# Splitting paired weight blocks as three tiles of 1024 columns and one of 512

## The chip, the cores and the metric

The kernel runs on one core of a Trainium2 chip. The time is the device time of one execution in microseconds (us), and what is compared is the median over several executions. A core has five engines, each with an instruction queue of its own that it works through in order: TensorE for matmuls (PE, and PEld for the weight loads that run beside them), VectorE (DVE), ScalarE (ACT), GpSimd (POOL) and SyncE (SP), which here issues transfers. The engines are held in step by semaphores. Which instruction stands where in a queue is settled when the program is built: a scheduler orders each engine's instructions from the order of the code and the buffers that are free, so a change of tile sizes can also move instructions that the change does not name.

## The reference, cut

One encoder layer on x of shape (1, 512, 1024) in float32: two gated branches (retention and a spatial gating unit) and a convolutional gated MLP.

```python
x1 = x  + rmsnorm_post_mix(sig(a_ret) * (Retention(h) @ w_ret_o) + sig(a_sgu) * (SGU(h) @ w_sgu_o))
y  = x1 + rmsnorm_post_ffn(ConvGatedMLP(rmsnorm_pre_ffn(x1)))      # h = rmsnorm_pre_mix(x)

def _sgu_branch(u, sv, ...):                 # u, sv, a_ret, a_sgu: columns of h @ w_in
    u = gelu(u); sv = layernorm(gelu(sv), ...)
    y = u * (einsum('gpq,bnqgc->bnpgc', w_spatial, chunks(sv)) + b_spatial.T)
    return y @ w_sgu_o
def _conv_gated_mlp(h, w_up, conv_w, conv_b, w_down):   # w_up: 1024 -> 2 x 2816
    hid = depthwise_conv(h @ w_up, conv_w) + conv_b
    ...                                                  # gate, then @ w_down: 2816 -> 1024
```

## The kernel before

All matrices are float32. A matmul runs on values split in a high and a low part: the high part is the value rounded to the TensorE's float32 format (made by a copy on ACT, L100), the low part what is left of it (a subtraction on VectorE, L119). Three matmuls per product add high × high, high × low and low × high. `split(hi, lo, src)` issues the copy and the subtraction.

**Weights.** They come as 146 blocks of 128 × 1024 (`wall`) by transfers into raw tiles (`raw_tile`, four buffers), and are split into tiles of a pool of nine buffers, `slot`, each 128 × 1088. A list `units` says in which order the pieces are needed; `w_get` hands out the next and prepares pieces ahead, as many as fit by `w_size` (in slots) into nine.

**Pairs.** For 20 pairs of weight blocks the product of two 512-deep, 2-block matrices is formed in Strassen's way, with 7 products in place of 8. Four pairs make the SGU's u (called U pairs), eight the two gates a_ret and a_sgu (gate pairs, `GATE0` to `GATE1`), eight belong to the up projection (`COUPLES`). Seven weight forms of 128 × 512 are needed per pair, out of the four quarters: B11, B21, T1, T2, T3, T4 and B22, each used by one product of 12 matmuls of 128 × 256 columns (L926). The T forms are sums of quarters made in `w_form`: T1 (L205) and T3 (L206) on VectorE, T2 (L208) and T4 (L211) on VectorE for U and up pairs and on GpSimd for gate pairs. T2 and T4 share half a raw tile. Each form is one split, and one slot holds its high and its low part.

**The pair's products.** Class `Pair` makes them in three parts: part 1 the products with B11, B21, T1 and T2; part 2 that with T3; part 3 those with T4 and B22. The result of the first product is copied out of PSUM on ACT at once, since the fourth product of the pair adds to the same PSUM bank. Between the parts other work is put by a table, `MIDDLE`, written out by hand: a row such as `U10 W2 U20 G10 U30 G20 U11` is part 1 of U pair 0, a weight block of an output projection (W, by `f_block`, L300 to L302), part 2 of U pair 0, part 1 of gate pair 0, and so on. Part 3 is followed by the activation (gelu, sigmoid; L1052, L1061), which loads a table on ACT when the function changes.

**After the pairs** come the conv, the down projection (L1372; its weights are split in `w_down` to dh and dl), and the last norm.

Of the kernel before, what the change touches and what calls it, by code (L numbers as in the profile page):

```python
# [13 lines left out]
ALU = mybir.AluOpType  # L14

P = 128
D = 1024
S = 512
# [9 lines left out]
SV0, U0, GATE0, GATE1 = 24, 32, 40, 72  # L28
# [8 lines left out]
UP0 = DOWN0 - 2 * NF  # L37
# [15 lines left out]
def tile_block(ctx: ExitStack, tc, xT, x, wall, par, cs, wsp, bsp, gpost, gffn, out):  # L53
    nc = tc.nc
# [6 lines left out]
    def nm(s):  # L61
        uid[0] += 1
        return f"{s}_{uid[0]}"
# [35 lines left out]
    def copy(o, i):  # L99
        return nc.scalar.activation(out=o, in_=i, func=AF.Copy)  # L100

    def two(t):
        return t.rearrange("p (n c) -> p n c", n=2)
# [8 lines left out]
    def as32(t):  # L112
        return t.bitcast(F32)
# [3 lines left out]
    def split(hi, lo, src):  # L117
        copy(hi, src)
        low[0] = nc.vector.tensor_sub(lo, src, as32(hi)).ins  # L119
# [2 lines left out]

    RES1 = NW - 22 - 44
    RES0 = RES1 - RES_OUT
    FORMS = ("B11", "B21", "T1", "T2", "T3", "T4", "B22")
    units = []
    i = 0
    while i < NW:
        pair = [(f, i) for f in FORMS]
        if i == SV0:  # L130
            units += [(f, k) for f in ("s11", "sT1", "sT2") for k in range(2)]
            units += [(f, k) for k in range(2) for f in ("s22", "sT3")]
            units += [(f, k) for f in ("s21", "sT4") for k in range(2)]
            i = U0
        elif i == U0:
            us, gs = ([[(f, k + n * m) for f in FORMS] for n in range(KD // 2)] for k, m in ((U0, 2), (GATE0, 4)))
            ws = [("blk", GATE0 + 4 * (n // 2) + 2 + n % 2) for n in range(KD)]
            for what, n in MIDDLE:
                units += {"W": lambda: ws[n : n + 1], "U1": lambda: us[n][:4], "U2": lambda: us[n][4:],
                          "G1": lambda: gs[n][:4], "G2": lambda: gs[n][4:]}.get(what, list)()  # L140
            i = GATE0 + 2 * KD
        elif GATE0 <= i < GATE1:
            units += pair[:4] + [("blk", i + 2)] + pair[4:] + [("blk", i + 3)]
            i += 4
        elif i == UP0 + 2 * COUPLES[0][0]:
            for a, b in COUPLES:
                pair = [(f, UP0 + 2 * a) for f in FORMS]
                units += pair[:4] + [("blk", UP0 + 2 * b)] + pair[4:] + [("blk", UP0 + 2 * b + 1)]
# [44 lines left out]

    def w_form(form, i):

        if form == "B11":
            a, b = raw_tile(), raw_tile()
            nc.sync.dma_start(a, wall[i])
            nc.sync.dma_start(b, wall[i + 1])
            w_raw["B11"], w_raw["B12"] = a[:, :S], a[:, S:]  # L200
            w_raw["B22"], w_raw["B21"] = b[:, :S], b[:, S:]
        elif form == "T1":
            t = raw_tile()
            w_raw["T1"], w_raw["T2"], w_raw["T3"], w_raw["T4"] = t[:, :S], t[:, S:], w_raw["B12"], t[:, S:]
            nc.vector.tensor_add(w_raw["T1"], w_raw["B11"], w_raw["B12"])  # L205
            nc.vector.tensor_add(w_raw["T3"], w_raw["B12"], w_raw["B22"])  # L206
            eng = nc.vector if i < GATE0 or i >= UP0 else nc.gpsimd
            eng.tensor_tensor(out=w_raw["T2"], in0=w_raw["T1"], in1=w_raw["B22"], op=ALU.add)  # L208
        elif form == "T4":
            eng = nc.vector if i < GATE0 or i >= UP0 else nc.gpsimd  # L210
            eng.tensor_tensor(out=w_raw["T4"], in0=w_raw["T2"], in1=w_raw["B21"], op=ALU.add)  # L211
        w = slot("wf", 0, 1088)
        lo, hi = w[:, AT_64 : AT_64 + S], w[:, S + AT_192 : 2 * S + AT_192]
        split(hi, lo, w_raw[form])
        return hi, lo

    def w_down(form, i):
# [60 lines left out]
    def w_unit(u):  # L278
        return w_block(u[1]) if u[0] == "blk" else (w_down if u[0] in "qt" else w_sv if u[0][0] == "s" else w_form)(*u)

    def w_size(u):
        return 2 if u[0] in ("blk", "q", "t") or u[0][0] == "s" else 1

    def w_get(look=LOOK):

        i = w_pos[0]
        w_pos[0] += 1
        room = 2 * look + (2 if w_size(units[i]) == 2 else 0)
        n = sum(w_size(u) for u in units[i : w_pos[1]])
# [18 lines left out]
    T0, T1 = slice(0, 256), slice(256, 512)  # L308
# [95 lines left out]
    for k in range(KD):  # L404
# [9 lines left out]
        wh, wl = w_get(1 if k < 4 else LOOK if k < KD - 1 else 2)  # L414
# [12 lines left out]
        for m in QK if k == KD - 1 else range(8):  # L427
            c = slice(m * P, (m + 1) * P)
# [36 lines left out]
    for t in range(NT):  # L465
        for n in range(2):
# [3 lines left out]
                out=xt, in_=xt, func=AF.Square, accum_out=ss[:, 4 * n + t : 4 * n + t + 1]  # L470
# [54 lines left out]
    raw, swapped = {}, {}  # L525
# [383 lines left out]
    class Pair:  # L909
# [6 lines left out]
            self.b = [ps() for _ in range(3)]  # L916
            self.two = in_turn if a is None else two

        def product(self, b, act, first, w=None):
            wh, wl = w or w_get()  # L920
            o = self.b[b][:, T0]
            for k in range(4):
                c = slice(k * P, (k + 1) * P)
                h_, l_ = act(k)
                for n, (w_, a_) in enumerate(((wh, h_), (wh, l_), (wl, h_))):
                    self.last = nc.tensor.matmul(  # L926
                        o, w_[:, c], a_, start=first and k == n == 0, stop=k == 3 and n == 2,
                        skip_group_check=True,
                    )
            pe_last[0] = self.last.ins  # L930
            return self.two(o)
# [10 lines left out]
        def part1(self):  # L942

            c0, c1 = self.t

            def second():
                o = self.product(1, self.x(4, T0), True)
                self.sum = v.tensor_add(two(c0[:, T0]), o, two(c0[:, T0])).ins

            o = self.product(0, self.x(0, T0), True)  # L950
            copy(two(c0[:, T0]), o)
            second()
            self.product(2, self.s("S1"), True)
            o = self.product(0, self.s("S2"), False)
            self.copied = copy(two(c1[:, T0]), o).ins
            if self.scale is not None:
                v.tensor_mul(c0[:, T0], c0[:, T0], self.scale[:, T0])

        def part2(self):
            c0, c1 = self.t  # L960
            o = self.product(0, self.s("S3"), False)
            copy(two(c1[:, T1]), o)
            v.tensor_sub(two(c1[:, T1]), self.two(self.b[2][:, T0]), two(c1[:, T1]))
            self.w = w_get(), w_get()

        def part3(self):
            c0, c1 = self.t
# [63 lines left out]
    r, us, gs = [], {}, {}  # L1031
# [299 lines left out]
    i = 0  # L1331
    while i < NF:
        if i in couples:
            p = Pair(None, lambda: tmp("c"), (h2h, h2l, h2forms))
            p.part1()
            o = [f_block(h2h, h2l, KD)]
# [5 lines left out]
        else:  # L1342
            o = []
# [75 lines left out]
    for j in range(DP):  # L1419
# [5 lines left out]
        if j in (3, 5):  # L1425
            w = w_get()
# [152 lines left out]
def _two(a):  # L1579

    b = _parts(a, 8, P).reshape(4, 2, P, 2, S)
    return np.stack([
        np.concatenate([b[:, 0, :, 0], b[:, 1, :, 0]], -1), np.concatenate([b[:, 1, :, 1], b[:, 0, :, 1]], -1),
    ], 1)


def _up(a):

    for i, _ in COUPLES:
        b, c = a[2 * i].reshape(P, 2, S), a[2 * i + 1].reshape(P, 2, S)  # L1590
        a[2 * i : 2 * i + 2] = np.stack([
            np.concatenate([b[:, 0], c[:, 0]], -1), np.concatenate([c[:, 1], b[:, 1]], -1),
        ])
    return a


# [82 lines left out]
```

## Time and profile before

| what | us |
| --- | --- |
| median of 3 runs (lowest, highest) | 783.61 (783.21, 783.69) |
| profiled execution, span | 782.6 |
| median less the span | 1.01 |
| ACT busy | 485.2 |
| POOL busy | 103.5 |

The runs list no separate time for the profiled execution; its span, from the first to the last recorded instruction, stands for it, and the median of the runs is 1.01 us longer. In the rows of the profile, "out<-in" names tiles as the program does, without their numbers; "x140" is a count, the number after the bar is the busy time in us, then the mean of one instruction in ns, then the idle time of the engine just before, with what ended it. L100 is line 100 of the kernel before.

### The profile page before, as it was taken

Reading aid. Unit: us, or ns where it says so; the run is one execution under the profiler, and the core shown is the slowest. Engines: PE = TensorE matmul, PEld = TensorE weight load, DVE = VectorE, ACT = ScalarE, POOL = GpSimd, SP = SyncE. Lnnn points to the kernel's source line nnn. Section 1 sums busy time; section 2 is a strip of 40 time slices with the busy share of each in tenths; the row PEclk is TensorE's granted clock in tenths of the full one; section 3 lists DMA queues with packets and bytes.
Section 4 is the critical chain, followed back from the end, with each engine's and each line's share of the span. In section 5 each row is a group of like instructions: output and inputs, shape, how many; then the busy total and the mean of one; then the engine's idle time right before and its main releaser. Section 6 shows DMA issues by size and latency. Waiting matters only on the chain.

```text
span 782.6 us, 13472 instructions
## 1 busy us (share of the span) xinstructions
PE 774.5 (99%) x5139; PEld 720.7 (92%) x5139; DVE 639.5 (82%) x1093; ACT 485.2 (62%) x878; POOL 103.5 (13%) x132
## 2 busy tenths in 40 slices
PE   9999999999999999999999999999999999999996
PEld 8888998998999999999998998999999998999996
DVE  6567987789789988877765679989999889886987
ACT  7555568688466766644454686657777568644542
POOL 0040001130021102033211200001111012200001
PEclk9999999999999999999999999999999999999998
DMA  8783224453223233233459120435555375733344
GB/s 288 271 246 102 81 82 162 108 122 108 81 91 126 82 122 121 83 110 106 138 171 337 54 81 28 124 107 141 142 148 149 108 199 111 171 114 107 109 162 162
DMA packets 35889, 104.80 MB, mean 134 GB/s; under 512 B 4400, under 2 KB 6320, under 8 KB 35824
## 3 DMA queue, kind: packets, MB, share of 16 engines
q1 hardware_dynamic: 27936, 87.81, 34.0%
q0 software_dynamic: 7024, 14.95, 9.0%
q10 hardware_dynamic: 864, 1.18, 0.4%
q8 instruction: 40, 0.66, 0.4%
q14 instruction: 25, 0.20, 0.1%
HBM read 91.34 MB, written 4.19 MB: 122 GB/s over the span
## 4 chain that ended last, share of the span: by engine, by line
PE 92%; DVE 3%; DMA 3%; issue 1%; ACT 0%; POOLq 0%; DVEq 0%; POOL 0%; ACTq 0%
PE ps L926 24%; PE ps L300 12%; PE ps L302 12%; PE ps L301 12%; PE ps L1372 7%; PE ps L755 5%; PE ps L634 4%; PE ps L636 4%; PE ps L635 4%; DMA raw<-wall 3%; PE ps L1109 2%; PE ps L1108 2%; PE ps L1107 2%; DVE dl L119 1%; PE ps L997 1%
## 5 line engine op out<-in xcount | busy, mean ns | idle before, releaser
L119 DVE TENSOR_TENSOR wl<-raw,wh 128x1024 fp32r<-128x1024 f32 (+1 forms) x84 | 96.0, 1152 | 54.3 <-issue 19.1
L100 ACT ACTIVATE wf<-raw 128x512 fp32r<-128x512 f32 x140 | 85.6, 625 | 67.3 <-PE ps L301 19.4
L926 PE MATMUL ps<-sh,wf 128*128 128x256 f32 x640 | 117.4, 276 | 0.1
L119 DVE TENSOR_TENSOR wf<-raw,wf 128x512 fp32r<-128x512 f32 x140 | 107.0, 774 | 9.2 <-ACT wf L100 8.6
L926 PEld LDWEIGHTS ps<-sh,wf 128*128 128x128 f32 x640 | 101.9, 192 | 1.1 <-ACT sig L100 0.5
L100 ACT ACTIVATE wh<-raw 128x1024 fp32r<-128x1024 f32 (+2 forms) x88 | 84.8, 977 | 28.5 <-DMA raw<-wall 14.0
L300 PE MATMUL ps<-h2h,wh 128*128 128x512 f32 (+1 forms) x256 | 90.6, 354 | 0.0
L301 PE MATMUL ps<-h2l,wh 128*128 128x512 f32 (+1 forms) x256 | 90.4, 353 | 0.0
L302 PE MATMUL ps<-h2h,wl 128*128 128x512 f32 (+1 forms) x256 | 90.4, 353 | 0.0
L926 PE MATMUL ps<-sl,wf 128*128 128x256 f32 x320 | 88.0, 275 | 0.0
L926 PEld LDWEIGHTS ps<-sl,wf 128*128 128x128 f32 x320 | 61.4, 192 | 0.4
L1372 PE MATMUL ps<-dh,fh 128*128 128x256 f32 x216 | 59.6, 276 | 0.3 <-DVE yy L1409 0.3
L1372 PE MATMUL ps<-dl,fh 128*128 128x256 f32 x216 | 59.5, 275 | 0.0
L1372 PE MATMUL ps<-dh,fl 128*128 128x256 f32 x216 | 59.4, 275 | 0.0
L100 ACT ACTIVATE dh<-raw 128x768 fp32r<-128x768 f32 (+1 forms) x36 | 33.6, 950 | 33.8 <-DVE raw L231 15.2
L302 PEld LDWEIGHTS ps<-h2h,wl 128*128 128x128 f32 x256 | 48.6, 190 | 5.1
L301 PEld LDWEIGHTS ps<-h2l,wh 128*128 128x128 f32 x256 | 48.6, 190 | 4.5
L300 PEld LDWEIGHTS ps<-h2h,wh 128*128 128x128 f32 x256 | 48.6, 190 | 4.5
L926 PE MATMUL ps<-xh,wf 128*128 128x256 f32 x288 | 52.2, 275 | 0.0
L636 PE MATMUL ps<-wh,xl 128*128 128x512 f32 x128 | 48.5, 379 | 0.0
L635 PE MATMUL ps<-wl,xh 128*128 128x512 f32 x128 | 48.5, 379 | 0.0
L634 PE MATMUL ps<-wh,xh 128*128 128x512 f32 x128 | 48.5, 380 | 0.0
(343 smaller groups left out, 2171.6 us busy)
## 6 DMA issues: line engine op xcount, KB each, us to landing
raw<-wall SPq DMA_DIRECT2D x144, 512.0 KB, 3.7
x<-x SPq DMA_DIRECT2D x24, 256.0 KB, 6.0
fl<-gp POOLq DMA_DIRECT2D x12, 256.0 KB, 3.8
swap<-qkraw POOLq DMA_DIRECT2D x16, 128.0 KB, 4.8
x<-x POOLq DMA_DIRECT2D x8, 256.0 KB, 2.3
fl<-fs POOLq DMA_DIRECT2D x8, 256.0 KB, 4.3
xT<-xT SPq DMA_DIRECT2D x7, 256.0 KB, 5.0
xT<-xT POOLq DMA_DIRECT2D x4, 256.0 KB, 4.1
```

Source lines behind the costliest of these rows:

```text
L100: return nc.scalar.activation(out=o, in_=i, func=AF.Copy)
L119: low[0] = nc.vector.tensor_sub(lo, src, as32(hi)).ins
L300: nc.tensor.matmul(o, ah, bh, start=start, stop=False, skip_group_check=skip)
L301: nc.tensor.matmul(o, ah, bl, start=False, stop=False, skip_group_check=skip)
L302: pe_last[0] = nc.tensor.matmul(o, al, bh, start=False, stop=stop, skip_group_check=skip).ins
L634: nc.tensor.matmul(acc[t], xh[k][:, c], turns(wh[:, f]), start=k == 0, stop=False)
L635: nc.tensor.matmul(acc[t], xh[k][:, c], turns(wl[:, f]), start=False, stop=False)
L636: part_end[0] = nc.tensor.matmul(acc[t], xl[k][:, c], turns(wh[:, f]), start=False, stop=k == KD - 1)
L755: nc.tensor.matmul(bank[t], a_[:, c], turns(w_[:, f]), start=first and k == i == 0, stop=last and k == 3 and i == 2, skip_group_check=True,)
L926: self.last = nc.tensor.matmul(o, w_[:, c], a_, start=first and k == n == 0, stop=k == 3 and n == 2, skip_group_check=True,)
L1107: nc.tensor.matmul(o, ah, turns(bh), start=k == 0, stop=False)
L1372: nc.tensor.matmul(o, a_[:, c], turns(w_[:, f]), start=j == t == i == 0, stop=j == DP - 1 and i == 2 and n not in (M2, M3, M4), skip_group ...
```

## The change

The seven forms become four pieces: `B1` (B11 and B21 side by side), `T12`, `T34` and `B22`. The first three are raw tiles of 128 × 1024 that are split whole, with a slot for the high and one for the low part; B22 stays as it was. A pair still takes seven slots. The host lays out the blocks so that B11 and the quarter of the second product stand side by side. T2 is summed on VectorE in all pairs (L206 after the change), T3 and T4 go into the first raw tile once B1 is split (L209, L210 after). T4 stays on GpSimd for gate pairs. A product no longer fetches its weights: `halves` fetches a tile for two products, and in part 2 the second half of T34 is kept for part 3.

```diff
-    FORMS = ("B11", "B21", "T1", "T2", "T3", "T4", "B22")
+    FORMS = ("B1", "T12", "T34", "B22")
...
-                units += {"W": lambda: ws[n : n + 1], "U1": lambda: us[n][:4], "U2": lambda: us[n][4:],
-                          "G1": lambda: gs[n][:4], "G2": lambda: gs[n][4:]}.get(what, list)()
+                units += {"W": lambda: ws[n : n + 1], "U1": lambda: us[n][:2], "U2": lambda: us[n][2:],
+                          "G1": lambda: gs[n][:2], "G2": lambda: gs[n][2:]}.get(what, list)()
...
-            units += pair[:4] + [("blk", i + 2)] + pair[4:] + [("blk", i + 3)]
+            units += pair[:2] + [("blk", i + 2)] + pair[2:] + [("blk", i + 3)]
...
     def w_form(form, i):
 
-        if form == "B11":
-            a, b = raw_tile(), raw_tile()
+        eng = nc.vector if i < GATE0 or i >= UP0 else nc.gpsimd
+        if form == "B1":
+            a, b = w_raw["a"], w_raw["b"] = raw_tile(), raw_tile()
             nc.sync.dma_start(a, wall[i])
             nc.sync.dma_start(b, wall[i + 1])
-            w_raw["B11"], w_raw["B12"] = a[:, :S], a[:, S:]
-            w_raw["B22"], w_raw["B21"] = b[:, :S], b[:, S:]
-        elif form == "T1":
-            t = raw_tile()
-            w_raw["T1"], w_raw["T2"], w_raw["T3"], w_raw["T4"] = t[:, :S], t[:, S:], w_raw["B12"], t[:, S:]
-            nc.vector.tensor_add(w_raw["T1"], w_raw["B11"], w_raw["B12"])
-            nc.vector.tensor_add(w_raw["T3"], w_raw["B12"], w_raw["B22"])
-            eng = nc.vector if i < GATE0 or i >= UP0 else nc.gpsimd
-            eng.tensor_tensor(out=w_raw["T2"], in0=w_raw["T1"], in1=w_raw["B22"], op=ALU.add)
-        elif form == "T4":
-            eng = nc.vector if i < GATE0 or i >= UP0 else nc.gpsimd
-            eng.tensor_tensor(out=w_raw["T4"], in0=w_raw["T2"], in1=w_raw["B21"], op=ALU.add)
-        w = slot("wf", 0, 1088)
-        lo, hi = w[:, AT_64 : AT_64 + S], w[:, S + AT_192 : 2 * S + AT_192]
-        split(hi, lo, w_raw[form])
+            w_raw["B22"], w_raw["B12"] = b[:, :S], b[:, S:]
+            raw = a
+        elif form == "T12":
+            raw = w_raw["t"] = raw_tile()
+            nc.vector.tensor_add(raw[:, :S], w_raw["a"][:, :S], w_raw["B12"])
+            nc.vector.tensor_add(raw[:, S:], raw[:, :S], w_raw["B22"])
+        elif form == "T34":
+            raw = w_raw["a"]
+            nc.vector.tensor_add(raw[:, :S], w_raw["B12"], w_raw["B22"])
+            eng.tensor_tensor(out=raw[:, S:], in0=w_raw["t"][:, S:], in1=raw[:, S:], op=ALU.add)
+        if form == "B22":
+            w = slot("wf", 0, 1088)
+            lo, hi = w[:, AT_64 : AT_64 + S], w[:, S + AT_192 : 2 * S + AT_192]
+            raw = w_raw["B22"]
+        else:
+            hi, lo = slot("wf", AT_192), slot("wf", AT_64)
+        split(hi, lo, raw)
         return hi, lo
...
     def w_size(u):
-        return 2 if u[0] in ("blk", "q", "t") or u[0][0] == "s" else 1
+        return 1 if u[0] == "B22" else 2
...
+        def halves(self):
+            hi, lo = w_get()
+            return [(hi[:, f], lo[:, f]) for f in (slice(0, S), slice(S, 2 * S))]
...
-            o = self.product(0, self.x(0, T0), True)
+            w = self.halves()
+            o = self.product(0, self.x(0, T0), True, w[0])
             copy(two(c0[:, T0]), o)
-            second()
-            self.product(2, self.s("S1"), True)
-            o = self.product(0, self.s("S2"), False)
+            second(w[1])
+            w = self.halves()
+            self.product(2, self.s("S1"), True, w[0])
+            o = self.product(0, self.s("S2"), False, w[1])
...
         def part2(self):
             c0, c1 = self.t
-            o = self.product(0, self.s("S3"), False)
+            w = self.halves()
+            o = self.product(0, self.s("S3"), False, w[0])
             copy(two(c1[:, T1]), o)
             v.tensor_sub(two(c1[:, T1]), self.two(self.b[2][:, T0]), two(c1[:, T1]))
-            self.w = w_get(), w_get()
+            self.w = w[1], w_get()
```

TensorE runs the same matmuls in the same order but for one place: three matmuls of an output projection (yh with wh and wl, L300 to L302 before), which stood ahead of the fourth product of the gate pair whose results are sig_645 and sig_646, stand behind it. On the other engines the order moves in many places; three are shown. Names with numbers are tiles; the second number is a running count and differs between the two programs.

The first place is ScalarE in the middle of that gate pair. The copy sig_645<-ps_647 brings the pair's first result out of PSUM; L1061 before and L1071 after is the sigmoid of an earlier pair. Before:

```order
L100 ACTIVATE wf_633_3599<-raw_617_3456 128x512
L100 ACTIVATE wf_634_3603<-raw_621_3491 128x512
L100 ACTIVATE yh_641_3657<-u_585_3248 128x512
L100 ACTIVATE wf_650_3670<-raw_618_3457 128x512
L1061 ACT_TABLE_LOAD
L1061 ACTIVATE sig_611_3435<-sig_611_3435 128x512
L100 ACTIVATE yh_643_3661<-u_586_3249 128x512
L1061 ACTIVATE sig_612_3436<-sig_612_3436 128x512
L100 ACTIVATE sig_645_3665<-ps_647_3667 128x256
```

After the change, the same stretch of ScalarE:

```order
L100 ACTIVATE wf_633_3548<-raw_617_3421 128x1024
L100 ACTIVATE yh_641_3603<-u_585_3206 128x512
L100 ACTIVATE wf_650_3616<-raw_618_3422 128x512
L100 ACTIVATE sig_645_3611<-ps_647_3613 128x256
L1071 ACT_TABLE_LOAD
L1071 ACTIVATE sig_611_3387<-sig_611_3387 128x512
L1071 ACTIVATE sig_612_3388<-sig_612_3388 128x512
```

The copy now stands ahead of the table load and the sigmoids, and the copies of two weight forms are one.

The second place is ScalarE in part 1 of the third U pair (results u_535 and u_536); L1052 before and L1062 after is the gelu of the second U pair. Before:

```order
L1052 ACT_TABLE_LOAD
L1052 ACTIVATE u_490_2565<-u_490_2565 128x512
L100 ACTIVATE sig_518_2759<-ps_519_2760 128x256
L100 ACTIVATE wf_533_2883<-raw_514_2751 128x512
L1052 ACTIVATE u_491_2566<-u_491_2566 128x512
L100 ACTIVATE wf_534_2887<-raw_523_2779 128x512
L100 ACTIVATE u_535_2890<-ps_537_2892 128x256
```

After, on ScalarE at the same place:

```order
L1062 ACT_TABLE_LOAD
L1062 ACTIVATE u_490_2547<-u_490_2547 128x512
L100 ACTIVATE sig_515_2728<-ps_516_2729 128x256
L1062 ACTIVATE u_491_2548<-u_491_2548 128x512
L100 ACTIVATE u_535_2860<-ps_537_2862 128x256
L100 ACTIVATE wf_533_2856<-raw_519_2732 128x1024
```

The copies of two forms, which stood ahead of the copy u_535<-ps_537, became one that stands behind it.

The third place is VectorE around the first weight tile of the second U pair. wf_475 and wf_481 are that pair's forms B11 and B21 before; wf_481 alone is the low part of its B1 after. raw_482 is where its T1 and T2 are summed, and wf_467, wf_468, wf_471 and wf_472 belong to the gate pair ahead of it. Before:

```order
L119 TENSOR_TENSOR wf_467_2378<-raw_465_2357,wf_467_2378 128x512
L119 TENSOR_TENSOR wf_468_2381<-raw_461_2322,wf_468_2381 128x512
L119 TENSOR_TENSOR wf_471_2414<-raw_465_2357,wf_471_2414 128x512
L963 TENSOR_TENSOR u_456_2302<-ps_459_2305,u_456_2302 128x256
L119 TENSOR_TENSOR wf_472_2431<-raw_462_2323,wf_472_2431 128x512
L119 TENSOR_TENSOR wf_475_2438<-raw_473_2434,wf_475_2438 128x512
L205 TENSOR_TENSOR raw_482_2462<-raw_473_2434 128x512
L119 TENSOR_TENSOR wf_481_2446<-raw_474_2435,wf_481_2446 128x512
L206 TENSOR_TENSOR raw_473_2434<-raw_473_2434,raw_474_2435 128x512
```

After, on VectorE from the gate pair's T3 sum (L209) to the low part of B1:

```order
L209 TENSOR_TENSOR raw_461_2329<-raw_462_2330 128x512
L119 TENSOR_TENSOR wf_467_2367<-raw_465_2363,wf_466_2366 128x1024
L119 TENSOR_TENSOR wf_471_2402<-raw_461_2329,wf_470_2401 128x1024
L205 TENSOR_TENSOR raw_482_2461<-raw_478_2427,raw_479_2428 128x512
L206 TENSOR_TENSOR raw_482_2461<-raw_482_2461,raw_479_2428 128x512
L973 TENSOR_TENSOR u_456_2296<-ps_459_2299,u_456_2296 128x256
L955 TENSOR_TENSOR sig_473_2422<-ps_476_2425,sig_473_2422 128x256
L966 TENSOR_TENSOR sig_473_2422<-sig_473_2422,rbc_103_567 128x256
L119 TENSOR_TENSOR wf_472_2405<-raw_462_2330,wf_472_2405 128x512
L119 TENSOR_TENSOR wf_481_2432<-raw_478_2427,wf_480_2431 128x1024
```

Both forms of the second U pair that were split apart are one subtraction of 1024 now, it stands behind the sums of that pair's T1 and T2, and the gate pair's T3 and T4 are one subtraction (wf_471), two rows behind the T3 sum.

In the down projection VectorE's order also moves between 650 and 690 us: sums of the last form of a tile (L230, L231 before) and of the low parts of the conv's results (fl) change places, so that ahead of the tile whose raw is raw_1306 fewer sums stand than before. From there to the end VectorE's order is as it was.

More of the change, by code (lines that the diff above doesn't have):

```diff
@@ L147, in tile_block @@
                 pair = [(f, UP0 + 2 * a) for f in FORMS]
-                units += pair[:4] + [("blk", UP0 + 2 * b)] + pair[4:] + [("blk", UP0 + 2 * b + 1)]
+                units += pair[:2] + [("blk", UP0 + 2 * b)] + pair[2:] + [("blk", UP0 + 2 * b + 1)]
             i = UP0 + 2 * COUPLES[-1][1] + 2
@@ L917, in __init__, with product @@
             self.two = in_turn if a is None else two
-        def product(self, b, act, first, w=None):
-            wh, wl = w or w_get()
+        def halves(self):
+            hi, lo = w_get()
+            return [(hi[:, f], lo[:, f]) for f in (slice(0, S), slice(S, 2 * S))]
+        def product(self, b, act, first, w):
+            wh, wl = w
             o = self.b[b][:, T0]
@@ L944, in part1, with second @@
             c0, c1 = self.t
-            def second():
-                o = self.product(1, self.x(4, T0), True)
+            def second(w):
+                o = self.product(1, self.x(4, T0), True, w)
                 self.sum = v.tensor_add(two(c0[:, T0]), o, two(c0[:, T0])).ins
-            o = self.product(0, self.x(0, T0), True)
+            w = self.halves()
+            o = self.product(0, self.x(0, T0), True, w[0])
             copy(two(c0[:, T0]), o)
-            second()
-            self.product(2, self.s("S1"), True)
-            o = self.product(0, self.s("S2"), False)
+            second(w[1])
+            w = self.halves()
+            self.product(2, self.s("S1"), True, w[0])
+            o = self.product(0, self.s("S2"), False, w[1])
             self.copied = copy(two(c1[:, T0]), o).ins
@@ L1582, in _two @@
     return np.stack([
-        np.concatenate([b[:, 0, :, 0], b[:, 1, :, 0]], -1), np.concatenate([b[:, 1, :, 1], b[:, 0, :, 1]], -1),
+        np.concatenate([b[:, 0, :, 0], b[:, 0, :, 1]], -1), np.concatenate([b[:, 1, :, 1], b[:, 1, :, 0]], -1),
     ], 1)
@@ L1589, in _up @@
     for i, _ in COUPLES:
[L1590 to L1593, printed above, removed]
+        a[2 * i + 1] = np.roll(a[2 * i + 1], S, -1)
     return a
```

## The prediction

> **What bounds the kernel now.** I read the page's busy line first, then the windows of 20 us, then the weight loads' waits.
>
> ```profile
> PE 774.5 (99%) x5139; PEld 720.7 (92%) x5139; DVE 639.5 (82%) x1093; ACT 485.2 (62%) x878; POOL 103.5 (13%) x132
> ```
>
> TensorE (PE) is busy for all but 1% of the span; VectorE (DVE) has 18% to spare. Where PE loses its 1% is in the windows (start:end and length, then busy us and instructions of PE, PEld, DVE, ACT, POOL, then granted clock, DMA share and GB/s):
>
> ```profile
> 0.00:20.00 20.00, 19.19 (x95) 16.27 (x96) 13.59 (x41) 13.84 (x21) 1.88 (x11) 1.00 0.82 284
> ...
> 240.00:260.00 20.00, 20.00 (x161) 19.41 (x160) 19.75 (x33) 15.36 (x26) 2.48 (x2) 1.00 0.19 63
> ...
> 320.00:340.00 20.00, 19.91 (x145) 18.60 (x144) 16.14 (x29) 11.33 (x19) 2.92 (x2) 1.00 0.33 106
> ...
> 720.00:740.00 20.00, 19.73 (x176) 19.49 (x175) 18.09 (x32) 9.09 (x23) 0.00 (x0) 1.00 0.32 107
> ...
> 760.00:780.00 20.00, 15.65 (x141) 15.45 (x139) 16.22 (x38) 5.47 (x18) 2.63 (x4) 0.95 0.47 160
> 780.00:782.60 2.60, 0.00 (x0) 0.00 (x0) 0.00 (x0) 0.00 (x0) 0.00 (x0) 0.50 0.42 148
> sum 782.60, PE 774.48 PEld 720.71 DVE 639.54 ACT 485.19 POOL 103.52; mean PE 19.36 PEld 18.02 DVE 15.99 ACT 12.13 POOL 2.59
> ```
>
> PE's idle time is 782.60 − 774.48 = 8.12 us, and five rows hold all of it: 0.81 at the start, 0.09, 0.27, 4.35 and 2.60 at the end. Every other window is full. The pairs that the change touches run from about 200 to 660 us; there PE idles 0.09 us. But a busy matmul can hide a late start, so I read what the weight loads (PEld) waited for (total us, times, longest):
>
> ```profile
> PEld L402 <- issue: 0.7, 1, 0.7
> PEld ps L926 <- ACT sig L100: 0.5, 1, 0.5
> PEld ps L1372 <- DVE yy L1409: 0.5, 1, 0.5
> PEld ps L420 <- ACT wh L100: 0.3, 1, 0.3
> PEld ps L420 <- ACT xh L337: 0.2, 1, 0.2
> PEld ps L926 <- ACT u L100: 0.2, 1, 0.2
> ```
>
> These six are all of them. L402 and L420 belong to the start and L1372 to the down projection. The pairs' products (L926) waited twice, 0.7 us in all, both times for a ScalarE (ACT) copy of a result out of PSUM, **never for a weight tile**. A change that makes weight tiles sooner takes from PE nothing that it waits for; it can win only by the side effect that those two copies move.
>
> **The two waits, sized by the spacing of the matmuls** (start, duration):
>
> ```profile
> 327.94 0.38 PE L301 MATMUL ps<-yl,wh 128*128 128x512 f32 x1
> 328.15 0.38 PE L302 MATMUL ps<-yh,wl 128*128 128x512 f32 x1
> 328.62 0.38 PE L926 MATMUL ps<-sh,wf 128*128 128x256 f32 x1
> ...
> 260.42 0.39 PE L926 MATMUL ps<-sh,wf 128*128 128x256 f32 x2
> ...
> 261.09 0.63 PE L926 MATMUL ps<-sh,wf 128*128 128x256 f32 x2
> ```
>
> At 328 the step from one matmul to the next grows from 0.21 to 0.47 us, a loss of about 0.25. At 261 two matmuls take 0.63 where two others took 0.39, a loss of 0.24. Together 0.5 us, against 0.7 by the waits. On ACT at these places:
>
> ```profile
> 325.11 1.28 ACT L1061 ACT_TABLE_LOAD   x1
> 326.40 0.64 ACT L1061 ACTIVATE sig<-sig 128x512 f32<-128x512 f32 x1
> 326.94 0.61 ACT L100 ACTIVATE yh<-u 128x512 fp32r<-128x512 f32 x1
> 327.67 0.64 ACT L1061 ACTIVATE sig<-sig 128x512 f32<-128x512 f32 x1
> 328.21 0.36 ACT L100 ACTIVATE sig<-ps 128x256 f32<-128x256 f32 x1
> ...
> 259.12 0.62 ACT L100 ACTIVATE wf<-raw 128x512 fp32r<-128x512 f32 x1
> ...
> 260.38 0.63 ACT L100 ACTIVATE wf<-raw 128x512 fp32r<-128x512 f32 x1
> 260.92 0.37 ACT L100 ACTIVATE u<-ps 128x256 f32<-128x256 f32 x1
> ```
>
> The copy of the pair's first result ends at 328.57, and at 261.29; the pair's fourth product accumulates in the same bank and waits for it. In the new order the copy at 328 stands ahead of the table load, so 3.1 us of ACT work (325.11 to 328.21) no longer precede it. The three matmuls of L300 to L302 that stood before the fourth product now stand behind it, so it is wanted some 0.64 us sooner, still 2.5 us to the good. At 261 the two copies of weights between the activations are gone (0.62 + 0.63); the copy would end near 260.0, over a us before it is wanted. I take both waits as gone: **−0.5 us** (bounds 0 and −0.7).
>
> **The splits.** Mean ns behind the bar:
>
> ```profile
> L100 ACT ACTIVATE wf<-raw 128x512 fp32r<-128x512 f32 x140 | 85.6, 625 | 67.3 <-PE ps L301 19.4 <-issue 17.3 <-DMA raw<-wall 10.9
> L100 ACT ACTIVATE wh<-raw 128x1024 fp32r<-128x1024 f32 x72 | 76.0, 1058 | 24.8 <-DMA raw<-wall 10.4 <-PE ps L636 8.8 <-PE ps L301 4.0
> ...
> L119 DVE TENSOR_TENSOR wf<-raw,wf 128x512 fp32r<-128x512 f32 x140 | 107.0, 774 | 9.2 <-ACT wf L100 8.6
> L119 DVE TENSOR_TENSOR wl<-raw,wh 128x1024 fp32r<-128x1024 f32 x72 | 88.5, 1229 | 52.6 <-issue 19.1 <-ACT wh L100 14.6 <-PE ps L926 6.3
> ...
> L205 DVE TENSOR_TENSOR raw<-raw 128x512 f32<-128x512 f32 x20 | 13.7, 685 | 0.5 <-DMA raw<-wall 0.5
> ...
> L208 POOL TENSOR_TENSOR raw<-raw,raw 128x512 f32<-128x512 f32 x8 | 13.3, 1660 | 90.6 <-DMA raw<-wall 74.2 <-DVE raw L205 16.4
> ...
> L211 POOL TENSOR_TENSOR raw<-raw,raw 128x512 f32<-128x512 f32 x8 | 11.4, 1422 | 27.4 <-DVE wf L119 27.4
> ```
>
> Twenty pairs: 140 copies of 512 become 60 of 1024 and 20 of 512, on ACT 60 × 1.058 + 20 × 0.625 = 76.0 us instead of 87.5. On DVE 60 × 1.229 + 20 × 0.774 = 89.2 instead of 108.4. The mean of 0.774 holds instructions that were stretched beside POOL; with an unstretched 0.685 it is 87.4 against 95.9. So DVE saves 8.5 to 19.2 us there and pays 8 × 0.685 = 5.5 for T2 of the gate pairs: 3 to 14 us of 639.5. The stretch that goes is seen here:
>
> ```profile
> 217.04 1.34 POOL L208 TENSOR_TENSOR raw<-raw,raw 128x512 f32<-128x512 f32 x1
> ...
> 217.16 1.77 DVE L206 TENSOR_TENSOR raw<-raw,raw 128x512 f32<-128x512 f32 x1
> ```
>
> A DVE sum that takes 0.685 elsewhere took 1.77 beside POOL's T2. All this is work of engines with time to spare, beside a PE that never waited for it. **Worth on the end of the span: 0** (bounds 0 and, through rival B, +4.0).
>
> **The waits it adds.** The first of a tile's two products could start after 0.625 + 0.774 = 1.40 us of copy and subtraction, and now after 1.058 + 1.229 = 2.29. For T34 of a gate pair, T4's sum on POOL now stands before both halves: 1.42 + 1.06 + 1.23 = 3.7 us from T3's sum to the ready tile. DVE, which takes its queue in order, has one subtraction (1.23) to do meanwhile and then waits up to 1.25 us per gate pair, with the next splits and the reads of PSUM behind it. What covers this is the lookahead of nine slots. The tightest place by count is the first tile (B1) of the second u pair: U0's T34 and B22 and G0's three tiles fill all nine; of the first two that come free G0's B22 takes one and B1's high part the other, and its low part waits for the end of G0's fourth product:
>
> ```profile
> 227.44 0.28 PE L926 MATMUL ps<-xh,wf 128*128 128x256 f32 x1
> ...
> 231.46 0.28 PE L926 MATMUL ps<-xh,wf 128*128 128x256 f32 x1
> ```
>
> The first row is the matmul behind that product, the second the first user of B1: 4.02 us, three products. The subtraction takes 1.23, so DVE may be 2.79 us late. The same order returns for the third u pair, used near 257.2. I take both as covered.
>
> **Sum.** Span 782.60 − 0.5 + 0 = 782.1. The median of the runs, 783.61, lies 1.01 above the span; with the same distance, **783.1 us**.
>
> **Rivals.**
>
> *C, nothing comes of it* (783.6 to 784.7). The copies are sooner, but the half us is lost again further on: the down projection waited 0.5 us for DVE's yy at L1409, a chain that the change leaves, and its order on DVE between 650 and 690 us is shuffled, with one tile there (dl) that has no slack:
>
> ```profile
> 683.77 1.22 DVE L119 TENSOR_TENSOR dl<-raw,dh 128x1024 fp32r<-128x1024 f32 x1
> ...
> 685.05 0.38 PE L1372 MATMUL ps<-dl,fh 128*128 128x256 f32 x1
> ```
>
> It ends 684.99, its matmul starts 685.05. One sum (0.685) put ahead of it costs most of its length, one and a half tiles 1.1 us: 783.6 + 1.1 = 784.7. For it: such a slack. Against it: the sums that stood between its forerunner and it now stand earlier. That the change does not lighten DVE at all falls here too, as PE does not ask for it.
>
> *B, the wider tiles come late* (slower, up to 787.1). One mechanism: DVE reaches the subtraction of B1 more than 2.79 us after the slot is free. For it: DVE is busy 19.75 of 20 us in 240:260, and ahead of B1's subtraction its queue has the new in-order wait for T34 (1.25) and the next pair's two sums (2 × 0.685 = 1.37); if two instructions beside POOL's T4 are stretched like the sum above (1.77 − 0.69 = 1.08 each), that is 4.8 us. Price: 4.8 − 2.79 = 2.0 us at each of two places, 783.1 + 4.0 = 787.1. Against it: all of this must meet after the slot is free, while most of it can run before, and DVE has less to do. The Trainium skill, "Perfetto Trace Analysis", section "Optimizing Scalar/DVE Operations", says that where ScalarE and VectorE aren't saturated but cause bubbles on other engines, breaking instructions up may let work finish sooner; the change does the reverse. By that rule B would come; the six rows of waits above show no bubble that a split caused, so the trace does not yet bear it out.
>
> *D, faster by over 0.2%* (below 782.0). It needs 1.57 us, and all waits in the list after the start's L402 sum to 1.7, of which the change can reach 0.7. Only a shorter end (the last two windows) would give it, and nothing there is edited.
>
> **How the numbers follow.** About 0.2%, or 1.57 us, is what a measurement here tells from no change; the three runs span 783.21 to 783.69. Forecast 0.50, C 0.33, B 0.14, D 0.03. Forecast and C lie within 0.2%: same 0.83, slower 0.14, faster 0.03. The range takes the forecast less its own spread (783.1 − 0.5, the scatter of the runs) and C's upper end with 0.2 of scatter: 782.6 to 784.9, which holds 0.83.
>
> **What would show it.** Right: no PEld wait for sig or u at L100; DVE groups of 60 at about 1.23 us and 20 near 0.7; on ACT 60 at about 1.06; POOL's T2 group gone; all windows from 20 to 720 us at 20.00. Wrong: a PE or PEld wait for wf of L119 near 231 or 257 (B), for dl near 685 or a longer one for yy (C), or a new wait for a PSUM copy behind a 1024 copy on ACT.

## The result, and the profile after

The changed kernel takes 787.72 us (median of 5 runs, 786.66 to 789.56), the kernel before 783.61 (5 runs, 783.21 to 784.51): a ratio of 1.0054, with a 95% interval of 1.0041 to 1.0066. It is slower by 4.1 us, or half a per cent, where 783.1 and no measurable change were forecast.

The page's busy line of the changed kernel:

```profile
PE 775.5 (99%) x5139; PEld 721.4 (92%) x5139; DVE 634.8 (81%) x1041; ACT 477.4 (61%) x818; POOL 92.9 (12%) x124
```

VectorE, ScalarE and GpSimd all have less to do than before (639.5, 485.2 and 103.5 us), and PE has the same matmuls. The span of the profiled execution grew from 782.6 to 785.9 us. The windows of 20 us, with the columns as in the prediction, say where PE stopped being full:

```profile
220.00:240.00 20.00, 19.62 (x173) 19.35 (x172) 14.16 (x21) 12.47 (x20) 0.00 (x0) 1.00 0.32 107
240.00:260.00 20.00, 19.72 (x152) 18.77 (x151) 18.96 (x30) 11.44 (x17) 1.28 (x1) 1.00 0.25 80
260.00:280.00 20.00, 18.66 (x145) 17.84 (x144) 18.74 (x28) 14.92 (x22) 1.53 (x1) 1.00 0.39 131
...
320.00:340.00 20.00, 20.00 (x148) 19.11 (x147) 17.73 (x27) 12.02 (x18) 1.61 (x1) 1.00 0.28 95
...
480.00:500.00 20.00, 19.89 (x116) 17.95 (x115) 20.00 (x30) 11.74 (x18) 0.00 (x0) 1.00 0.29 101
...
720.00:740.00 20.00, 19.58 (x173) 19.20 (x172) 16.82 (x29) 9.83 (x24) 0.00 (x0) 1.00 0.27 94
```

320:340, which had lost 0.09 us, is full now, as forecast. But the three windows from 220 to 280, all full before, lose 0.38, 0.28 and 1.34 us. What the weight loads waited for in the changed kernel, all rows:

```profile
PEld ps L933 <- ACT u L100: 2.1, 2, 1.5
PEld ps L933 <- ACT c L100: 1.1, 3, 0.4
PEld L405 <- issue: 0.7, 1, 0.7
PEld ps L933 <- ACT sig L100: 0.5, 1, 0.5
PEld ps L1382 <- DVE yy L1419: 0.5, 1, 0.5
PEld ps L1382 <- DVE e L1418: 0.3, 1, 0.3
PEld ps L423 <- ACT xh L340: 0.3, 1, 0.3
```

The rows sum to 5.5 us against 2.4 before; the 3.1 more are nearly all of the 3.3 us by which the span grew. Again **no row of the pairs names a weight tile**. All new waits of the pairs (L933, which was L926) are for copies out of PSUM: u and sig in the middle stage, c in the up projection.

The longest of them is at 262 us. PE, ScalarE and SP at that place in the changed kernel (start, duration, and in brackets the idle time before):

```profile
262.24 0.27 PE L933 MATMUL ps<-sh,wf 128*128 128x256 f32 x1
263.85 0.38 PE L933 MATMUL ps<-sh,wf 128*128 128x256 f32 x1 [1.33 <-ACT u L100]
...
253.84 2.71 ACT L100 ACTIVATE wf<-raw 128x512 fp32r<-128x512 f32 x3
256.46 0.37 ACT L100 ACTIVATE sig<-ps 128x256 f32<-128x256 f32 x1
259.72 1.06 ACT L100 ACTIVATE wh<-raw 128x1024 fp32r<-128x1024 f32 x1 [2.89 <-DMA raw<-wall]
260.81 1.28 ACT L1062 ACT_TABLE_LOAD   x1
262.10 0.63 ACT L1062 ACTIVATE u<-u 128x512 f32<-128x512 f32 x1
262.64 0.36 ACT L100 ACTIVATE sig<-ps 128x256 f32<-128x256 f32 x1
262.90 0.62 ACT L1062 ACTIVATE u<-u 128x512 f32<-128x512 f32 x1
263.42 0.37 ACT L100 ACTIVATE u<-ps 128x256 f32<-128x256 f32 x1
...
256.03 0.33 SPq L176 DMA_DIRECT2D raw<-wall  x1
...
255.32 0.69 DVE L119 TENSOR_TENSOR wf<-raw,wf 128x512 fp32r<-128x512 f32 x1
```

Read it from the end. (The row of 253.84 holds three copies in a line, B22's of 512 and two of 1024.) PE waits for the copy of u that ends at 263.79. That copy had nothing wrong of its own: it stood in ScalarE's queue behind a weight block's copy (wh), which waited 2.89 us for its transfer. The transfer was issued at 256.03, as soon as its raw tile was free, and the tile came free when VectorE had made the low part of B22 of the pair ahead (255.32 to 256.0). In the kernel before the same steps, and the copy of the block, were:

```profile
250.50 1.28 DVE L119 TENSOR_TENSOR wf<-raw,wf 128x512 fp32r<-128x512 f32 x2
...
251.24 0.33 SPq L176 DMA_DIRECT2D raw<-wall  x1
...
255.96 1.05 ACT L100 ACTIVATE wh<-raw 128x1024 fp32r<-128x1024 f32 x1
257.03 1.28 ACT L1052 ACT_TABLE_LOAD   x1
```

The first of those two subtractions is the same low part. The block's copy stood ahead of the table load there too, but it waited for nothing. The split is some 4.8 us later after the change, so the transfer is too, and ScalarE's queue stands. The wait near 235 us begins in the same way: its block's transfer went out at 228.37 instead of 225.53, and the block's copy waited 3.12 us; behind it an activation of u also waited 1.10 us for VectorE. That is one reading of one trace; the experiments test its links.

### The profile page after: what moved, and what is told of

The parts are those of the page before. It is cut to its first block, busy times and chain, and to the rows that moved or that the text cites. A ratio compares the mean times of both kernels' runs of the same rounds, so it can differ in the third digit from the quotient of the medians.

```text
span 785.9 us, 13354 instructions
## 1 busy us (share of the span) xinstructions
PE 775.5 (99%) x5139; PEld 721.4 (92%) x5139; DVE 634.8 (81%) x1041; ACT 477.4 (61%) x818; POOL 92.9 (12%) x124
## 4 chain that ended last, share of the span: by engine, by line
PE 56%; DVE 6%; DMA 2%; ACT 1%; issue 1%; POOLq 0%; DVEq 0%; POOL 0%
PE ps L933 19%; PE ps L1382 8%; PE ps L303 7%; PE ps L304 7%; PE ps L305 7%; PE ps L1117 2%; PE ps L1118 2%; PE ps L1119 2%; DMA raw<-wall 2%; PE ps L1398 1%; DVE dl L119 1%; PE ps L1007 1%; ACT h L1205 1%; DVE cv L1260 1%; DVE wl L119 0%
## 5 line engine op out<-in xcount | busy, mean ns | idle before, releaser
L933 PE MATMUL ps<-sh,wf 128*128 128x256 f32 x640 | 118.2, 276 | 2.1 <-ACT u L100 1.7
L933 PEld LDWEIGHTS ps<-sh,wf 128*128 128x128 f32 x640 | 102.3, 192 | 3.4 <-ACT u L100 2.1
L100 ACT ACTIVATE wf<-raw 128x1024 fp32r<-128x1024 f32 x80 | 75.1, 946 | 41.0 <-DVE raw L206 20.1
L119 DVE TENSOR_TENSOR wf<-raw,wf 128x1024 fp32r<-128x1024 f32 x80 | 92.6, 1158 | 8.0 <-ACT wf L100 6.3
L933 PE MATMUL ps<-sl,wf 128*128 128x256 f32 x320 | 88.1, 275 | 0.0
L933 PEld LDWEIGHTS ps<-sl,wf 128*128 128x128 f32 x320 | 61.4, 192 | 0.4
L933 PE MATMUL ps<-xh,wf 128*128 128x256 f32 x288 | 52.2, 276 | 0.0
## 6 DMA issues: line engine op xcount, KB each, us to landing
x<-x SPq DMA_DIRECT2D x24, 256.0 KB, 5.8
fl<-gp POOLq DMA_DIRECT2D x12, 256.0 KB, 4.9
x<-x POOLq DMA_DIRECT2D x8, 256.0 KB, 2.4
fl<-fs POOLq DMA_DIRECT2D x8, 256.0 KB, 3.3
xT<-xT SPq DMA_DIRECT2D x7, 256.0 KB, 5.8
xT<-xT POOLq DMA_DIRECT2D x4, 256.0 KB, 3.5
```

Source lines behind the costliest of these rows:

```text
L933: self.last = nc.tensor.matmul(o, w_[:, c], a_, start=first and k == n == 0, stop=k == 3 and n == 2, skip_group_check=True,)
```

## The experiments

Two theories were put up. **Q (queue)**: copies out of PSUM stand on ScalarE behind splits that wait for late transfers, since raw tiles come free later under the new tiles. **L (length)**: a copy of 1024 takes 1.06 us in front of them, where one of 512 took 0.63. A third, P, put the loss on the sums of T2 that moved to VectorE. Ratios are to the kernel before, run on the same chip beside them, with its median of 783.7 to 783.9.

**1. Two splits of 512 in the new tiles.** After the change with

```diff
-        split(hi, lo, raw)
+        for f in (slice(0, S), slice(S, 2 * S)) if form != "B22" else (slice(0, S),):
+            split(hi[:, f], lo[:, f], raw[:, f])
```

> The new tiles, units and slots, but each tile of 1024 is split by two copies and two subtractions of 512. Theory L (length: a copy of 1024 on ScalarE takes 1.06 us in front of the copies out of PSUM, where 512 took 0.63): most of the loss comes back, 783.6 to 784.8, and the PE waits for u, sig and c go. Theory Q (queue: the copies out of PSUM stand behind splits that wait for a late weight transfer, because raw buffers come free later under the new tiles): still 786.5 or more, and the u wait near 262 stays over 1 us.

Measured: 786.08 us (11 runs), ratio 1.0029 (1.0019 to 1.0038). Neither theory had it right: 1.6 of the 4.1 us come back, 2.3 stay over the 783.77 of the kernel before. The sig wait and the u wait near 235 are gone, the u wait near 262 remains, with its transfer at 254.68:

```profile
PEld ps L934 <- ACT c L100: 1.3, 3, 0.5
PEld ps L934 <- ACT u L100: 1.3, 1, 1.3
```

**2. A slot for every form.** The new raw tiles, sums and order of preparing, but each form of 512 with a slot of its own:

```diff
-        else:
-            hi, lo = slot("wf", AT_192), slot("wf", AT_64)
+        if form != "B22":
+            out = []
+            for f in (slice(0, S), slice(S, 2 * S)):
+                w = slot("wf", 0, 1088)
+                lo, hi = w[:, AT_64 : AT_64 + S], w[:, S + AT_192 : 2 * S + AT_192]
+                split(hi, lo, raw[:, f])
+                out.append((hi, lo))
+            return out
...
-            hi, lo = w_get()
-            return [(hi[:, f], lo[:, f]) for f in (slice(0, S), slice(S, 2 * S))]
+            return w_get()
```

> The new raw tiles and units, but every form of 512 gets a slot of its own for its high and low part and is split by itself, as before the change; tiles are still prepared two forms at a time. Theory L: as with two splits of 512 in one tile, 783.6 to 784.8. Theory Q, if it is the slots (one slot comes free only when both halves of a tile are used): near 783.6 to 784.5 too, and below the run with two splits by over 1 us. Theory Q, if it is the preparing two by two and the order of the sums: 786 or more.

Measured: 783.87 us (11 runs), ratio 0.9998 (0.9989 to 1.0007). The whole loss is gone. Its splits are of the same size as in run 1, so the 2.2 us between the two are the slots. How they act is read from the program: a slot that holds the high parts of two forms comes free only when both products are done. The trace shows the next link: the middle blocks' transfers go out at 225.02 and 249.95, against 226.98 and 254.68 in run 1, and the u wait is gone. VectorE's sums of T2 and the preparing by two are still in this kernel; with these slots they cost nothing that shows.

**3. T2 back on GpSimd.** `eng.tensor_tensor` in place of `nc.vector.tensor_add` for T2.

> The change with T2 of the gate pairs summed on GpSimd again. Theory P (the added VectorE sums delay the splits): 785 or less. Theories Q and L: no gain, 787 to 789, as the eight sums (0.69 us each) are no part of the waits that they name and the sum on GpSimd takes 1.66 us and stretches VectorE's.

Measured: 788.46 us (5 runs), ratio 1.0062 (1.0044 to 1.0080). Theory P falls.

**4. B22 prepared ahead of T34.**

```diff
-    FORMS = ("B1", "T12", "T34", "B22")
+    FORMS = ("B1", "T12", "B22", "T34")
...
+            w_22 = w_get()
             w = self.halves()
...
-            self.w = w[1], w_get()
+            self.w = w[1], w_22
```

> The change with B22 prepared ahead of T34, so that the raw tile with B22 comes free sooner. Theory Q: the transfers of the blocks after it are issued some 3 us sooner than 228.4 and 256.0 us, the u waits (2.1 us) go for the most part, and the time is 785.0 to 786.3. Theory L: no gain, 787 to 788.5.

Measured: 787.53 us (5 runs), ratio 1.0050 (1.0032 to 1.0068). The transfers went out at 226.32 and 254.42, 2.1 and 1.6 us sooner, where some 3 were expected, and the u wait fell from 2.1 to 1.1 us. The median did not follow. The profile doesn't say why: it is of the fastest of the five runs (786.51). A wait for dl (0.2) appeared there in the down projection and that for e grew from 0.3 to 0.6, but that for c fell from 1.1 to 0.5. The link from transfer to wait holds, the size of the gain was missed.

**5. Only the block's split moved.** The split of an output projection's block that was prepared ahead is issued after the next pair's first copy out of PSUM. Tiles and slots stay; `flush` issues the splits held back.

```diff
-                with behind():
-                    split(hi, lo, raw)
+                def late():
+                    with behind():
+                        split(hi, lo, raw)
+                if GATE0 <= i < GATE0 + 2 * KD:
+                    w_late.append((i, late))
+                else:
+                    late()
...
-            copy(two(c0[:, T0]), o)
+            done = copy(two(c0[:, T0]), o).ins
+            with tc.issue_after(done):
+                flush()
```

> The change, with one thing moved: the split of a block of the first output projection (wh, wl) that has been prepared ahead stands behind the next pair's copy of its first result out of PSUM. Theory Q (the copies out of PSUM wait on ScalarE behind a block's copy that waits for its late transfer): the u waits near 235 and 262 (2.1 us) go, the block's transfers stay as late as 228.4 and 256.0, and the time is 785.2 to 786.3. If the lateness acts by another way: no change, 787 to 788.5.

Measured: 786.99 us (5 runs), ratio 1.0036 (1.0024 to 1.0048). The u and sig waits are gone altogether, though the first of the two transfers went out as late as in the change (228.36) and the second at 253.48. So what held PE near 235 was the place in ScalarE's queue; near 262 an earlier transfer may have helped. The time fell by only 0.7 us, which the two intervals don't separate from the change. A block now came too late itself, and a wait for dl (0.6) is new in the down projection:

```profile
PEld ps L318 <- DVE wl L119: 1.3, 1, 1.3
PEld ps L946 <- ACT c L100: 1.1, 3, 0.4
```

**6 and 7. The change in one stage alone.** The old forms for the U and gate pairs with the new tiles in the up projection, and the reverse. Both are the two kernels put together, each pair taking the code of its own.

> Forms as before the change for the U and gate pairs, the new tiles for the eight up pairs alone. From the steps between matmuls that the two traces lost and won: up stage 0.27 + 0.17 + 0.18 and 0.32 in the down projection, less 0.21 gained there: 784.3 to 784.8. If the stages were tied (a late start handed on): outside of that.

> The new tiles for the U and gate pairs alone, forms as before for the up pairs. By the same steps 0.54 + 0.44 + 0.10 + 1.50 lost and 0.49 won: 2.1 to 2.9 us over the kernel before, 785.9 to 786.7.

Measured: new tiles in the up projection alone 786.16 us (7 runs, ratio 1.0025, 1.0015 to 1.0035); in the middle alone 786.58 (5 runs, 1.0037, 1.0025 to 1.0049). The middle came out as its waits said. The up projection cost 2.4 where 0.5 to 1.0 was expected: beside c (1.1 us) its trace has waits in the down projection for dl and e (0.6 each) that the changed kernel's trace did not show in that size. The two do not add up to 4.1 (2.4 + 2.8 = 5.2).

**8. The kernel before with eight slots.** `bufs=8` for the slots, and 8 for 9 in the lookahead.

> The kernel before with eight weight slots in place of nine and as much less lookahead. Theory Q with slots as its root: a slot that comes free later is enough to bring the same waits, so u, sig or c waits on PE of over 1 us in all appear, the middle blocks' transfers are issued later than 225.5 and 251.2, and the time is 785 to 788. If the order of the new sums or the length of 1024 is the root: 783.4 to 784.3, as before.

Measured: 790.17 us (6 runs, 787.54 to 792.91), ratio 1.0078 (1.0054 to 1.0101), slower than expected. Three runs lie at 787.5 to 788.3 and three at 792.1 to 792.9; the profile is one of the upper three. Without any wide form the same sort of waits arises, for copies out of PSUM, beside a tile (dl) that is late in the down projection:

```profile
PEld ps L1372 <- DVE dl L119: 3.3, 2, 3.1
PEld ps L926 <- ACT c L100: 1.3, 2, 0.6
PEld ps L301 <- DVE st L119: 1.1, 1, 1.1
PEld ps L926 <- ACT sig L100: 0.9, 1, 0.9
```

Eight slots with less lookahead are thus too few. But the run does not repeat the change's loss at its place: between 200 and 280 us PE waits for nothing. The two transfers went out at 227.50 and 253.12, which is later, as expected, but PE itself was 1.5 us behind there (the 16 matmuls of L997 start at 246.17 in place of 244.68), so the transfers fell back by only 0.5 and 0.4 us against the work.

**9 and 10. Ten slots.** Paid for with two of six scratch tiles (`tmp`), in the changed kernel and in the one before.

> The change with ten weight slots in place of nine (and lookahead to ten), paid for with two of six small scratch tiles. If coarse slots are the root: the u waits of 2.1 us fall below 1, the middle blocks' transfers are issued sooner than 228.4 and 256.0 us, and the time is 784 to 786. If length alone is the root: 787 or more.

> The kernel before with ten slots and two scratch tiles fewer. It waits for no weight tile, so a tenth slot gives nothing: 783.4 to 784.3. Under 782.3 would say that PE did wait for slots in a way that the list of waits does not show; over 784.6 would say that the scratch tiles matter and that the two runs above are to be read with that cost.

Measured: 808.14 us (5 runs, ratio 1.0317) and 800.61 (4 runs, 1.0214). Both expectations fall, and badly. In the changed kernel the u wait did fall below 1, to 0.7 us, but waits for c grew to 9.0 and for sig to 4.4; the kernel before got u waits of 2.9 us. In both, waits of 4.9 and 5.1 us for kz arise in the retention branch, before the middle stage. Run 12 below has the same four scratch tiles with nine slots and takes 791.10 us, so some 17 of the 20.4 us belong to the tenth slot and its lookahead. Why they cost so much stays open. Late transfers are not shown to be the reason: the first block's went out at 232.27 in the changed kernel, but PE was 6.9 us behind there (the 16 matmuls of L1007 start at 251.96 in place of 245.07), so against the work it was 3.0 us sooner than in the change.

**11 to 13. A fifth raw tile**, paid for with the same two scratch tiles; a control with the four scratch tiles alone; and the kernel before with five raw tiles and four scratch tiles.

```diff
-        return sb.tile([P, 1024], F32, tag="raw", bufs=4, name=nm("raw"))
+        return sb.tile([P, 1024], F32, tag="raw", bufs=5, name=nm("raw"))
...
-        return sb.tile(list(shape), F32, tag="tmp", bufs=6, name=nm(n))
+        return sb.tile(list(shape), F32, tag="tmp", bufs=4, name=nm(n))
```

> The change with five raw tiles in place of four, paid for with the same two scratch tiles; nine slots. Theory Q, if the raw tile that comes free late is a needed link from slots to the late transfer: the middle blocks' transfers go out several us sooner, the u waits go, 784.5 to 786. If ScalarE is late by splits that wait for slots whatever the transfers do: 787 or more.

> The change with four scratch tiles in place of six, four raw tiles, nine slots. If the scratch tiles cause the c waits of the run with five raw tiles: c waits of about 5.5 us, seven steps of 0.6 us in the up stage, u waits of 2 us still in the middle, 792 to 796. If the fifth raw tile caused them: no more than 1.3 us of c waits, 787 to 790.

> The kernel before with five raw tiles and four scratch tiles. If scratch tiles cost 5 us in the up stage whatever the forms: 787 to 791, and the two waits of 0.7 us in the middle go or stay below 0.7. If they don't: 782.8 to 784.2.

Measured: five raw tiles 790.96 us (4 runs, ratio 1.0090), the control 791.10 (4 runs, 1.0095), the kernel before with both edits 787.43 (6 runs, 1.0057). Each expectation was missed in part: five raw tiles took the u waits away but did not bring the time down, the control has its c waits but stayed just below 792, and the kernel before got slower without any c wait. The first two differ in the raw tile alone. The control's waits of the pairs, and its windows:

```profile
PEld ps L933 <- ACT c L100: 5.7, 8, 0.8
PEld ps L933 <- ACT u L100: 2.1, 2, 1.6
...
PEld ps L933 <- ACT sig L100: 0.4, 1, 0.4
...
220.00:240.00 20.00, 19.62 (x173) 19.35 (x172) 14.19 (x22) 12.03 (x19) 0.00 (x0) 1.00 0.33 107
240.00:260.00 20.00, 19.77 (x155) 18.89 (x154) 19.39 (x31) 12.00 (x17) 1.27 (x1) 1.00 0.25 80
260.00:280.00 20.00, 18.61 (x144) 17.78 (x144) 18.58 (x28) 14.83 (x23) 1.53 (x1) 1.00 0.42 132
```

With the fifth raw tile:

```profile
PEld ps L933 <- ACT c L100: 5.5, 8, 0.8
...
220.00:240.00 20.00, 20.00 (x175) 19.86 (x174) 17.47 (x28) 14.15 (x21) 0.42 (x1) 1.00 0.35 112
240.00:260.00 20.00, 20.00 (x164) 19.49 (x163) 19.59 (x31) 14.16 (x22) 0.85 (x1) 1.00 0.31 94
260.00:280.00 20.00, 20.00 (x159) 19.36 (x158) 18.98 (x29) 13.32 (x20) 1.27 (x1) 1.00 0.28 90
```

The u and sig waits of the pairs are gone and the three windows are full, with copies of 1024 and slots of two forms both in place. The middle blocks' transfers went out at 223.25 and 246.84, against 227.82 and 255.41 in the control. ScalarE's own waits between 220 and 265 us say why. In the control its copy of a block waited 6.1 us for transfers; with five raw tiles no such row is left:

```profile
ACT wh L100 <- DMA raw<-wall: 6.1, 2, 3.1
```

The c waits are the price of four scratch tiles with the wide forms: the control has them too, and with the narrow forms the same two edits bring none. The time of the fifth raw tile is no better because it loses elsewhere what it wins: waits of 1.2 us each for wh and wl of another projection, which the kernel before with five raw tiles shows as well (1.3 and 1.2). No kernel here beats the one before.

**14. The change once more**, for a second profile.

> The change itself once more, for a second profile. The u, sig and c waits of the middle and up stages come back within 0.2 us each if they follow from the order of the queues; what differs between the two profiles (start, down projection) is scatter of the transfers.

Measured: 791.54 us in a single run, above all five of the result. The c waits are again 1.1 us; u waits are 2.5 and sig has no row, so together 2.5 against 2.6, though not each within 0.2. Waits for dl, for wl in the down projection and for wh at the start came on top (0.3, 0.5, 0.7). The middle stage's loss came back, so it belongs to the kernel; the rest differs from run to run.

## Why the prediction was wrong

- **What bounds the kernel**: right, and it stayed so. PE is the bound, and no wait for a form's weight tile appeared in the changed kernel's list.
- **The two waits, −0.5 us**: half right. The copy at 328 moved ahead of the table load, the window is full, the wait is gone. At 261 the two copies of weights are gone from ahead of the u copy, as the order said, but the copy that "would end near 260.0" ended at 263.79. The order gave what stands ahead, not when it runs: ahead of the table load stood a block's copy that now waited for a transfer. In place of 0.24 won, 1.3 us were lost there. The prediction's own list of signs had this one, a new wait for a PSUM copy behind a copy of 1024 on ACT, but no rival and no price stood behind it.
- **The splits**: right in kind. ScalarE's wide copies of forms took 1.053 us (60) against an assumed 1.058, VectorE's subtractions 1.317 against 1.229, and VectorE saved 4.7 us in all, inside the 3 to 14:

```profile
L119 DVE TENSOR_TENSOR wf<-raw,wf 128x1024 fp32r<-128x1024 f32 x60 | 79.0, 1317 | 7.9 <-ACT wf L100 6.3 <-PE ps L304 1.3
```

- **"Worth on the end of the span: 0"** is the step that failed. I followed each late split to one reader only, the matmul that uses the tile, and found slack there. A split has a second reader: the transfer that waits for its raw tile. From there the lateness went through ScalarE's queue to a copy out of PSUM, and that had no slack, as the two waits of the trace before already showed at the same kind of place. In place of 0, the splits and their slots cost some 3.8 us: halving the length in the same slots gives back 1.6 (run 1), and a slot for each form the other 2.2 (run 2). The two were undone in this order only, so the parts hold for this order. Run 5 shows the queue (near 235 us), runs 11 and 12 that the raw tile is the link. This explains the middle stage (2.6 us of waits); the up projection's share is open, as said below.
- **The added waits**: no wait for wf came, so rival B did not come as written, but it was near. At the third U pair the subtraction of B1 began 2.87 us after the matmul behind the fourth product (253.99 to 256.86), where the bound was 2.79, and ended at 258.08, 0.25 before its first user at 258.33. That B's time (up to 787.1) lies close to the measured one is luck. I also put T4's sum behind T3's; T4 is T2 plus B21 and doesn't need T3: a sum on GpSimd ran from 217.68 while T3's ran on VectorE from 217.47 to 218.15. C's wait for dl near 685 did not come.
- **The rule cited with B**: the Trainium skill, "Perfetto Trace Analysis", section "Optimizing Scalar/DVE Operations", says that where ScalarE and VectorE aren't saturated but cause bubbles on other engines, breaking instructions up may let work finish sooner. Run 1 agrees, by 1.6 us at the same work. That is less than half of the loss.
- **Sum**: the distance of 1.01 us between span and median mixed two executions. All listed runs of the changed kernel lie 1.75 to 1.83 above their own span, so by estimate the profiled execution before took about 784.4, 0.8 above its median. That would be why the spans differ by 3.3 and the medians by 4.1.

Open: which of slots, length and order makes the c waits of the up projection (1.1 us after the change, 1.3 in run 1, 0.5 in run 2); why the change in the up projection alone costs 2.4 us; and why the down projection's waits for dl and e come and go between runs.

## What to carry to other kernels

When a change makes a tile later, list everyone who waits for it: the engine that reads the result, and also the transfer that waits for the buffer its source lies in. Then ask, for each late instruction, what stands behind it in an in-order queue. Here an engine that is 61% busy held up TensorE for 1.5 us, because a copy at the head of its queue waited 2.9 us for data.

Two forms in one buffer halve the instructions, but the buffer comes free at the later of its two uses. Where buffers are just enough (one slot fewer, with less lookahead, cost 6.4 us here), that is a loss of buffers, and it should be priced as one. More buffers are not the cure by themselves: a tenth slot made both kernels slower, and what freed TensorE in the middle stage was one more of the raw tiles that the transfers waited for.
